# Opening the second feed-forward: seven-part chunks in place of two plain ones, and other places for the combinations of its input

## Chip, cores and metric

The kernel runs on one core of one Trainium2 chip. The metric is the device time of one execution in microseconds; the time before is the median of three runs.

## What is computed

A two-layer encoder over 768 tokens (two sequences, 512 and 256) with model width 1024, all in float32. Layer 0 mixes tokens by windowed attention, layer 1 by a gated width-3 convolution. Each layer then has the feed-forward that this change touches, and a gated input embedding:

```python
h = rms_norm(x, norm_mlp[i])
x = x + jnp.square(jax.nn.relu(h @ mlp_w_up[i])) @ mlp_w_down[i]
gate = jax.nn.sigmoid(rms_norm(x, norm_ple[i]) @ ple_w_gate[i])
x = x + (p[i] @ ple_w_proj[i]) * gate
```

Here i is the layer, mlp_w_up is 1024 x 4096 and mlp_w_down 4096 x 1024.

## The kernel before

**Precision.** Each float32 operand is split in two parts, a rounded high part (written by ScalarE, named ...hi) and the rest (written by VectorE as a subtraction, named ...lo). A product of two operands is three matmuls: high by high, high by low, low by high. So every tile of weights costs ScalarE a copy and VectorE a subtraction, and every input as well.

**Chunks and seven parts.** Tokens lie on the free axis in two halves of 384 (H). An up-projection chunk is a pair of weight tiles of 128 x 1024. Done plainly (plain_product), a chunk is 2 x 2 blocks of output by 8 blocks of depth by 3 matmuls, 96 matmuls of 128 x 384. Done in seven parts (seven_parts, a Winograd form of Strassen's scheme over 2 x 2 blocks), it is seven products of 12 matmuls, 84 in all. For that, sums of weights (Weights7: sums32, sums14) and of inputs are formed on VectorE. The inputs of the seven products are x11, x21 and x22 (blocks of the input) and t1 to t4 (their combinations). Plain chunks need x12 too, and no combinations. Norm7.block writes the x parts of one of the eight 128-row blocks m of the input, and Norm7.combine(m), m from 0 to 3, forms t1 to t4 of blocks m and m + 4: two copies q (ScalarE), four sums (t13, t42), two high parts t (ScalarE), two low parts t (VectorE).

**The norm.** h is x times a gain, times a reciprocal root per token (rstd). The gain is put in when the parts are made; rstd is applied after the matmuls. It needs acc, the sum of squares of all eight blocks: a split of acc (ah, al), four matmuls by ones (ss), logarithm, exponential, square and a Newton step. The logarithm needs another set of ScalarE's functions, so a table is loaded ahead of it (ACT_TABLE_LOAD, L647).

**Where the change lies.** In layer 1 the convolution ends with the output projection (project_add): eight products of 48 matmuls each, block order 0, 4, 1, 5, 2, 6, 3, 7. After each, VectorE adds it to x and Norm7.block runs for that block. first_chunk gives the function behind(i) that is called after each product: it fetches and splits the first weights of the feed-forward and runs combine for the first pairs of blocks. After the eighth product mlp takes the 16 up chunks u; two chunks make a group g, whose down products follow one chunk later. PLAIN = 2, 2 says that each layer's first two chunks are plain: they need no combinations, so the last two combine calls are run beside them (early = 2). Chunks 2 and later are in seven parts.

**Order.** The operations are recorded, and a planner with its own costs sets the order on each engine; each engine works through its list in that order. Tiles lie in numbered slots of the on-chip memory, which lists at the end of the program hand out (xs1, act1, spare, held1). Weights land in three shared tiles (wraw), the copies in two pairs (whi, wlo) and one more each (zhi/zlo, vhi/vlo). The names of products: in plain chunks p; in seven parts a, b, c and d, where c and d begin as ScalarE's copies of a. Each wlo, zlo and vlo is L874 on VectorE, each whi, zhi and vhi L863 on ScalarE.

Of the kernel before, what the change touches and what calls it, by code (L numbers as in the profile page):

```python
# [456 lines left out]
def trunk_kernel(ctx: ExitStack, tc: tile.TileContext, a: dict, out: bass.AP):  # L457
# [118 lines left out]
    def slot(i, name, dt=F32R, n=T):  # L576

        return home(slots if i < 32 else more, n, dt, f"S{i}", name)
# [20 lines left out]
    class Norm:  # L599
# [34 lines left out]
        aside = temp  # L634
# [80 lines left out]
    class Norm7(Norm):  # L715
# [2 lines left out]

        def __init__(self, i, name, places, aside, acc, rstd=None, apart=None):
            super().__init__(i, name, places, acc, rstd)  # L720
            self.free, self.x12 = list(places), list(aside)
            self.apart = self.free if apart is None else list(apart)
            self.xs = {k: {} for k in (*QS7.values(), "x12")}

# [3 lines left out]
        def block(self, m, xb):  # L728
            g = gain(self.i, m)
            if m < KB // 2:  # L730
                for j, t in enumerate((self.place(), slot(self.x12.pop(0), "x12"))):
                    src = xb[:, j * H : j * H + H]
                    hi, lo = t[:, :H], t[:, H:]
                    act.activation(hi, src, AF.Copy, scale=g)
                    dve.scalar_tensor_tensor(lo, src, g, hi.bitcast(F32), ALU.mult, ALU.subtract)
                    self.xs[("x11", "x12")[j]][m] = hi, lo
            else:
                hi, lo = self.place(), self.place()
                act.activation(hi[:], xb, AF.Copy, scale=g)
                dve.scalar_tensor_tensor(lo[:], xb, g, hi[:].bitcast(F32), ALU.mult, ALU.subtract)  # L740
                for j, k in enumerate(("x21", "x22")):
                    self.xs[k][m - KB // 2] = hi[:, j * H : j * H + H], lo[:, j * H : j * H + H]
            self.square(m, xb)
# [144 lines left out]
    def product7(ps, w, key, xs, start, step=P, col=0):  # L888

        hi, lo = w.w[key]  # L890
        rhs = xs[QS7[key]]
        ks = [(slice(step * i + col, step * i + col + P), rhs[i]) for i in range(512 // step)]
        terms = [(hi[:, c], p) for c, ps_ in ks for p in ps_] + [(lo[:, c], ps_[0]) for c, ps_ in ks]
        for i, (a, b) in enumerate(terms):
            pe.matmul(ps, lhsT=a, rhs=b, start=start and i == 0, stop=i == len(terms) - 1, skip_group_check=True)  # L895
# [242 lines left out]
    psum = ctx.enter_context(tc.tile_pool(name="ps", bufs=1, space=PSUM))  # L1138
# [724 lines left out]
    def up_chunk(l, u):  # L1863
        f = 4 * (u // 2) + u % 2
        return Weights7(a["up"][l, f], a["up"][l, f + 2], plain=u < PLAIN[l])


    PLAIN = 2, 2

    def run(steps, n=None):  # L1870

        for _ in range(len(steps) if n is None else n):
            steps.pop(0)()
# [31 lines left out]
        run(combined)  # L1905
        run(steps)

    def first_chunk(chunk, norm, early):


        w = []

        def behind(i):
            if i == 6:
                w.append(chunk(0))
                w[0].split("direct")
            if i == 7:
                w[0].split("second")
            if i % 2 and i // 2 < early:
                run(norm.combine(i // 2))  # L1920
            if i == 7:
                w.append(chunk(1))
                w[1].split("second")

        return w, behind

    ET = mybir.EngineType

# [65 lines left out]
        v.low("second")  # L1994
        return parts, v

    def seven_parts(w, xs, make, then, first, late, out, soon=False, apart=False):

        w.low("s32")
        w.split("s14")
        if not first:
            late()
        v = make()
        more7 = isinstance(v, Weights7)
        a = bank("A", "a")[:, :H]
        product7(a, w, "w11", xs, True)
        if not first:
            late()  # L2010
        c = bank("A" if first else "C", "c")[:, :H]
        act.activation(c, a, AF.Copy)
        if more7 and soon:
            v.sums32()
        late(3 if first else 1)
        w.split("w22")
        late()
        b = bank("A" if first else "B", "b")[:, :H]
        product7(b, w, "s3", xs, True)
        p = big("p")[:, :H]  # L2020
        act.activation(p, b, AF.Copy)
        if more7 and not soon:
            v.sums32()
        product7(a, w, "s2", xs, False)
        d = bank("B", "d")[:, :H]
        act.activation(d, a, AF.Copy)
        late(2)
        if more7:
            v.sums14(0 if apart else None)
            v.high("s32")  # L2030
        late()
        product7(c, w, "w12", xs, False)
        if more7:
            v.high("direct")
        product7(a, w, "s1", xs, False)
        out.y22(a, p)
        if more7 and apart:
            v.sums14(1)
# [33 lines left out]
    def mlp(l, norm, nxt, w, w1, places, early, spare, product=None, follow=None):  # L2072


        xs = norm.xs
        r = parts = None
# [55 lines left out]
        def late(n=1):  # L2132

            for _ in range(n):
                if pend:
                    pend.pop(0)()

        def up_plain(u, w, make, then):

            nonlocal r, parts  # L2140

            ps = [both(f"p{i + 1}", {0: "AA", 1: "BC"}.get(u, "AA")[i]) for i in range(2)]
            y1 = y2 = None
# [12 lines left out]
            for n, (i, ks, sides) in enumerate(plain_order(u or parts)):  # L2156
                plain_product(ps, w, xs, i, ks, sides)
                if n == 0:
                    if u:
                        v.split("direct")  # L2160
                        v.sums32()
                    elif product:
                        v.split("direct")
                        run(c[-1], 2)
                        norm.table()
                        ss = norm.sum_squares(psum, parts=parts, tag="C")
                    else:
                        parts = norm.acc_parts()
                        two(*c)
                        norm.table()  # L2170
                elif n == 1:
                    if u:
                        v.high("s32")
                        rects((0, 1), (0, 0))
                        v.low("s32")
                        v.sums14()
                        late(len(pend))
                    else:
                        if not product:
# [28 lines left out]
        def up(u, w, make, then):  # L2208

            out = Squares()  # L2210
            v = seven_parts(w, xs, make, then, u == PLAIN[l], late, out, u == PLAIN[l])
            pend.extend(acts_of(u, out.y1, out.y2, (out.y2, out.y1)))
            return v

# [727 lines left out]
    ls = [xs2[7]] + ys[:5] + [ys[7], ys[5]]  # L2942
    free = [i for i in xs2 if i not in hs + ls] + wide + [xs0[16], ys[6]]

    xs1 = free[:20] + hs
    act1 = ls[:7] + free[20:26] + ls[7:]

    n3 = Norm7(1, "mix1", xs2, x12, act0[9])
    w2, behind = first_chunk(conv_chunk, n3, 1)
    ple(n2, n3, act0[10:13], behind, w)  # L2950

    n4 = Norm7(3, "mlp1", xs1, act1[7:11], act1[11])
    w1, behind = first_chunk(lambda u: up_chunk(1, u), n4, 2)
    mixer_conv(n3, *w2, 1, n4, wide, xs0[16], ys, hs, ls, behind)
    spare = [xs1[i] for i in (17, 10, 11, 20, 0, 7, 14, 12, 13, 21, 22, 23, 24, 25)]
    held1 = [xs1[i] for i in (1, 2, 8, 9, 15, 16, 18, 19, 26, 27)] + act1[:2] + xs1[3:7] + act1[2:3]
    n5 = Norm(5, "ple1", held1[:16], held1[16])
    mlp(1, n4, n5, *w1, act1, 2, spare)
    free = act1[3:7] + act1[7:] + [spare[i] for i in (4, 11, 0, 1, 7, 8, 2, 3, 9, 10, 5, 6, 12, 13)]
    last_stage(  # L2960
        n5,
# [83 lines left out]
```

## Time and profile before

| | |
|---|---|
| median of 3 runs | 1625.18 us (1625.07 to 1625.44) |
| profiled execution, its own time | 1625.47 us |
| its span, first to last instruction | 1623.6 us |
| granted TensorE clock | 0.998 |
| busy share of the span: TensorE / VectorE / ScalarE / GpSimd | 99 / 84 / 58 / 6 % |

The profiled execution took 0.29 us more than the median, and 1.87 us of its time lie outside its span. In rows of the time line the columns are start, length, engine, line, operation, output and inputs, shapes, count, and in brackets the idle time before it and what ended it. PE is TensorE, PEld its loading of weights, DVE VectorE, ACT ScalarE, POOL GpSimd and SP the queue of transfers. Neighbouring instructions of one engine overlap a little, so two times matter: the length of a row, and its pace, which is the distance from its start to the start of the next row.

### The profile page before, as it was taken

The numbers are of one execution on the slowest core, as the hardware profiler recorded it, in microseconds if no ns is written. First come the engines' busy times: TensorE is split into PE (matmuls) and PEld (weight loads), VectorE is DVE, ScalarE is ACT, GpSimd is POOL, SyncE is SP. The second block draws the span as 40 slices with busy tenths as digits, with TensorE's granted clock in tenths as the row PEclk, the third lists the DMA queues.
The fourth block names the chain that finished last, engine by engine and source line by source line (L and its number), as shares of the span: only waits on it lengthen the run. The fifth ranks groups of instructions, "written<-read, shape, count | busy, mean of one in ns | idle before, by whom it ended". The sixth has DMA issues, their size and how long they took to land.

```text
span 1623.6 us, 24456 instructions
## 1 busy us (share of the span) xinstructions
PE 1613.7 (99%) x9325; PEld 1569.2 (97%) x9325; DVE 1368.3 (84%) x2225; ACT 946.6 (58%) x1497; POOL 99.5 (6%) x158
## 2 busy tenths in 40 slices
PE   9999999999999999999999999999999999999997
PEld 7988889999999999999999999999999999999987
DVE  7579988988888888998898777687888978889985
ACT  7478887655545555556663434565555545546655
POOL 0001000010110110100000000000110110010000
PEclk9999999999999999999999999999999999999999
DMA  8745312332443343323312211212343343342232
GB/s 305 204 131 152 98 37 88 114 91 82 114 108 95 97 103 94 103 70 103 104 62 78 70 69 70 78 66 67 100 106 93 103 106 86 94 117 78 84 121 88
DMA packets 61649, 163.71 MB, mean 101 GB/s; under 512 B 7611, under 2 KB 23355, under 8 KB 61532
## 3 DMA queue, kind: packets, MB, share of 16 engines
q1 hardware_dynamic: 47564, 143.14, 26.7%
q0 software_dynamic: 13824, 18.88, 7.1%
q8 instruction: 73, 1.20, 0.3%
q14 instruction: 44, 0.36, 0.1%
q10 hardware_dynamic: 144, 0.13, 0.0%
HBM read 123.85 MB, written 9.96 MB: 82 GB/s over the span
## 4 chain that ended last, share of the span: by engine, by line
PE 94%; DVE 3%; ACT 1%; issue 1%; DMA 0%; DVEq 0%; ACTq 0%
PE a L895 36%; PE b L895 9%; PE mm L435 9%; PE p L2064 6%; PE mm L557 6%; PE d L895 5%; PE c L895 5%; PE B L895 4%; PE C L895 4%; PE gate L2439 3%; PE O L435 2%; PE S L435 2%; PE gate L557 2%; PE pt L435 1%; PE vp L435 1%
## 5 line engine op out<-in xcount | busy, mean ns | idle before, releaser
L874 DVE TENSOR_TENSOR zlo<-sum,zhi 128x1024 fp32r<-128x1024 f32 x70 | 85.7, 1224 | 74.3 <-ACT zhi L863 74.1
L2271 POOL DMA_DIRECT2D x<-p x96 | 84.2, 878 | 976.5 <-DVE x L2232 779.7
L863 ACT ACTIVATE whi<-sum 128x1024 fp32r<-128x1024 f32 x70 | 74.4, 1063 | 103.8 <-PE a L895 92.6
L863 ACT ACTIVATE vhi<-wraw 128x512 fp32r<-128x512 f32 x70 | 44.3, 633 | 144.4 <-PE B L895 62.2
L895 PE MATMUL a<-xs,whi 128*128 128x384 f32 x608 | 117.6, 334 | 0.0
L895 PE MATMUL b<-t,zhi 128*128 128x384 f32 x560 | 113.6, 334 | 0.0
L895 PE MATMUL a<-t,zhi 128*128 128x384 f32 x560 | 113.5, 334 | 0.0
L895 PE MATMUL a<-t,whi 128*128 128x384 f32 x560 | 113.5, 334 | 0.0
L895 PE MATMUL a<-act,whi 128*128 128x384 f32 x512 | 109.3, 334 | 0.0
L895 PEld LDWEIGHTS a<-xs,whi 128*128 128x128 f32 x608 | 106.5, 188 | 0.0
L863 ACT ACTIVATE whi<-wraw 128x1024 fp32r<-128x1024 f32 x76 | 80.2, 1056 | 33.9 <-PE C L895 19.2
L895 PEld LDWEIGHTS b<-t,zhi 128*128 128x128 f32 x560 | 98.6, 188 | 0.0
L895 PEld LDWEIGHTS a<-t,zhi 128*128 128x128 f32 x560 | 98.5, 188 | 0.0
L895 PEld LDWEIGHTS a<-t,whi 128*128 128x128 f32 x560 | 98.5, 188 | 0.0
L863 ACT ACTIVATE zhi<-sum 128x1024 fp32r<-128x1024 f32 x70 | 74.3, 1062 | 39.6 <-PE a L895 37.0
L874 DVE TENSOR_TENSOR wlo<-wraw,whi 128x1024 fp32r<-128x1024 f32 x76 | 92.8, 1221 | 0.0
L895 PEld LDWEIGHTS a<-act,whi 128*128 128x128 f32 x512 | 90.6, 188 | 0.0
L874 DVE TENSOR_TENSOR wlo<-sum,whi 128x1024 fp32r<-128x1024 f32 x70 | 85.3, 1219 | 0.9 <-ACT whi L863 0.9
L435 PE MATMUL mm<-xs_mix,whi 128*128 128x512 f32 (+1 forms) x320 | 80.0, 339 | 0.0
L2232 DVE TENSOR_TENSOR x<-x,a 128x384 f32<-128x384 f32 x128 | 67.5, 549 | 12.0 <-PE a L895 12.0
L782 ACT ACTIVATE t<-y 128x768 fp32r<-128x768 f32 x64 | 53.6, 838 | 37.2 <-DVE y L778 22.2
L895 PE MATMUL a<-act,wlo 128*128 128x384 f32 x256 | 64.9, 334 | 0.0
(376 smaller groups left out, 4428.9 us busy)
## 6 DMA issues: line engine op xcount, KB each, us to landing
wraw<-in_up SPq DMA_DIRECT2D x64, 512.0 KB, 3.5
wraw<-in_down SPq DMA_DIRECT2D x64, 512.0 KB, 3.4
x<-p POOLq DMA_DIRECT2D x96, 192.0 KB, 3.0
wraw<-in_w_in SPq DMA_DIRECT2D x24, 512.0 KB, 3.4
wraw<-in_gate SPq DMA_DIRECT2D x16, 512.0 KB, 3.5
wraw<-in_w_q SPq DMA_DIRECT2D x8, 512.0 KB, 4.5
wraw<-in_w_out SPq DMA_DIRECT2D x8, 512.0 KB, 3.4
x_in<-in_x SPq DMA_DIRECT2D x8, 384.0 KB, 7.1
```

Of the source, the lines that this page charges most:

```text
L435: return f(*args, **kw)
L557: pe.matmul(t, lhsT=w, rhs=x[:, o:e], start=first and i == 0 and j == 0, stop=last and i == n - 1 and j == 2)
L782: act.activation(t[0][:], (self.q1, self.q2)[i][:], AF.Copy)
L863: act.activation(hi[:], src, AF.Copy)
L874: dve.tensor_tensor(lo[:], src, hi[:].bitcast(F32), ALU.subtract)
L895: pe.matmul(ps, lhsT=a, rhs=b, start=start and i == 0, stop=i == len(terms) - 1, skip_group_check=True)
L2064: pe.matmul(ps[i][o], lhsT=wt[:, c], rhs=xs[f"x{h + 1}{1 + o}"][m][part], start=k == 0 and j == 0, stop=k == KB - 1 and j == 2,)
L2232: dve.tensor_tensor(t[:, o : o + H], t[:, o : o + H], f, op)
L2271: pool.dma_start(low[i][:, o : o + H], p[:, i * H : i * H + H], accum_op=ALU.add)
L2439: pe.matmul(ps.t[:, o : o + n], lhsT=a_, rhs=b_, start=begin and i == 0 and j == 0, stop=end and i == len(terms) - 1 and j == 2,)
```

## The change

In the second layer the first two up chunks become seven-part chunks too (PLAIN = 2, 0). The combinations of block pairs 0, 1 and 2 are run during the output projection (early = 3), that of pair 3 after the first product of chunk 0 (the new function rooted, passed as opened), together with the norm's root. x12 is no longer made in this layer (aside = None), so four blocks have half as many parts to write. Only chunk 0's weights are prepared during the output projection, now with their sums; chunk 1 follows from inside chunk 0. The lists of slots are handed out anew.

```diff
         def __init__(self, i, name, places, aside, acc, rstd=None, apart=None):
             super().__init__(i, name, places, acc, rstd)
-            self.free, self.x12 = list(places), list(aside)
+            self.free, self.x12 = list(places), list(aside or ())
+            self.first = "x11", "x12"
+            if aside is None:
+                self.first = "x11",
...
-    PLAIN = 2, 2
+    PLAIN = 2, 0
...
-    def first_chunk(chunk, norm, early):
+    def first_chunk(chunk, norm, early, plain=True):
         w = []
+
+        def seven(i):
+            if i == 6:
+                w.append(chunk(0))
+            if i == 7:
+                w[0].sums32()
+                w[0].sums14()
+                w[0].high("s32")
+                w[0].split("direct")
+            if i % 2 and i // 2 < early:
+                run(norm.combine(i // 2))
...
-        return w, behind
+        return w, behind if plain else seven
...
         a = bank("A", "a")[:, :H]
         product7(a, w, "w11", xs, True)
+        if opened:
+            opened()
...
+        def rooted():
+
+            nonlocal r
+            for m in todo:
+                run(norm.combine(m))
+            sq = norm.acc_parts()
+            norm.table()
+            run(norm.rstd_steps(psum, norm.sum_squares(psum, parts=sq, tag="A")))
+            r = norm.r
...
-            v = seven_parts(w, xs, make, then, u == PLAIN[l], late, out, u == PLAIN[l])
+            first = u and u == PLAIN[l]
+            v = seven_parts(w, xs, make, then, first, late, out, first, opened=None if u else rooted)
...
-    xs1 = free[:20] + hs
-    act1 = ls[:7] + free[20:26] + ls[7:]
+    xs1 = free[:24] + hs[:4]
+    act1 = ls[:7] + hs[4:8] + free[24:26] + ls[7:]
...
-    n4 = Norm7(3, "mlp1", xs1, act1[7:11], act1[11])
-    w1, behind = first_chunk(lambda u: up_chunk(1, u), n4, 2)
+    n4 = Norm7(3, "mlp1", xs1, None, act1[11])
+    w1, behind = first_chunk(lambda u: up_chunk(1, u), n4, 3, False)
```

How the order moves is shown at three places. The numbers tell tiles of one name apart.

On TensorE, before, around the norm's sums in the first plain chunk: p_11087 and p_11090 are its two token halves, xs_11106 and xs_11116 the high and low part of the last input block, 7.

```order
L2064 MATMUL p_11087<-xs_11106,zhi 128x384
L2064 MATMUL p_11090<-xs_11106,zhi 128x384
L2064 MATMUL p_11087<-xs_11116,zhi 128x384
L2064 MATMUL p_11090<-xs_11116,zhi 128x384
L2064 MATMUL p_11087<-xs_11106,zlo 128x384
L2064 MATMUL p_11090<-xs_11106,zlo 128x384
L666 MATMUL ss<-ah,ones 128x384
L666 MATMUL ss<-al,ones 128x384
```

On TensorE now, at the same sums in chunk 0: t_11119 and t_11133 are the high and low part of pair 3's first combinations, t_11152 the high part of its second, xs_11126 and xs_11158 the parts of block 7.

```order
L899 MATMUL c<-xs_11126,whi 128x384
L666 MATMUL ss<-ah,ones 128x384 x2
L899 MATMUL b<-t_11133,zhi 128x384
L899 MATMUL b<-t_10672,zlo 128x384
L899 MATMUL b<-t_10817,zlo 128x384
L899 MATMUL b<-t_10974,zlo 128x384
L899 MATMUL b<-t_11119,zlo 128x384
L666 MATMUL ss<-al,ones 128x384 x2
L899 MATMUL a<-t_11152,zhi 128x384
L899 MATMUL c<-xs_11158,whi 128x384
```

The products b, a and c are no longer each in one piece: the matmuls that read pair 3 stand behind those that do not. 41 matmuls stand between the last one of the output projection and the one that reads t_11152.

On ScalarE, before, from the weights that wait for the last product of the output projection:

```order
L863 ACTIVATE whi<-wraw 128x1024
L626 ACTIVATE sq<-x 128x768
L739 ACTIVATE xs_11106<-x,vec 128x768
L498 ACTIVATE ah<-acc_mlp_10592 128x768
L647 ACT_TABLE_LOAD
L751 ACTIVATE q<-x,vec 128x768
L782 ACTIVATE t_11141<-q 128x768
L782 ACTIVATE t_11153<-q 128x768
```

And on ScalarE now, from the same place (whi of chunk 0's second sums) to the copy d:

```order
L867 ACTIVATE whi<-sum 128x1024
L755 ACTIVATE q<-x,vec 128x768
L626 ACTIVATE sq<-x 128x768
L2029 ACTIVATE c<-a 128x384
L786 ACTIVATE t_11119<-q 128x768
L743 ACTIVATE xs_11126<-x,vec 128x768
L498 ACTIVATE ah<-acc_mlp_10592 128x768
L647 ACT_TABLE_LOAD
L786 ACTIVATE t_11152<-q 128x768
L685 ACTIVATE ln<-ss,eps 128x384 x2
L867 ACTIVATE whi<-wraw 128x1024
L2038 ACTIVATE p<-b 128x384
```

The copies q and c and one part t now stand ahead of ah and of the table; the other part t stands right behind the table. After p come zhi<-sum and d<-a.

On VectorE, before, from the last addition to x:

```order
L1849 TENSOR_TENSOR x<-x,mm 128x384 x2
L874 TENSOR_TENSOR wlo<-wraw,whi 128x1024
L627 TENSOR_TENSOR acc_mlp_10592<-acc_mlp_10592,sq 128x768
L740 SCALAR_TENSOR_TENSOR xs_11116<-x,vec,xs_11106 128x768
L499 TENSOR_TENSOR al<-acc_mlp_10592,ah 128x768
L773 TENSOR_TENSOR q<-q 128x384
```

And on VectorE now, with one row ahead of that addition, a sum of chunk 1's weights:

```order
L840 TENSOR_TENSOR sum<-wraw 128x512
L1853 TENSOR_TENSOR x<-x,mm 128x384 x2
L878 TENSOR_TENSOR wlo<-sum,whi 128x1024
L777 TENSOR_TENSOR q<-q 128x384
L841 TENSOR_TENSOR sum<-sum,wraw 128x512
L627 TENSOR_TENSOR acc_mlp_10592<-acc_mlp_10592,sq 128x768
L781 SCALAR_TENSOR_TENSOR q<-q 128x384
L792 TENSOR_TENSOR t_11133<-q,t_11119 128x768
L782 SCALAR_TENSOR_TENSOR q<-q 128x384
L499 TENSOR_TENSOR al<-acc_mlp_10592,ah 128x768
L744 SCALAR_TENSOR_TENSOR xs_11158<-x,vec,xs_11126 128x768
L792 TENSOR_TENSOR t_11165<-q,t_11152 128x768
```

The combinations of pair 3 and a sum of weights now stand between the last addition and al. SP's list holds the same transfers in the same sequence. In the last stage of the program a few neighbouring instructions trade places (TensorE's transposes, and steps of the gates on VectorE and ScalarE).

More of the change, by code (lines that the diff above doesn't have):

```diff
@@ L730, in block @@
             if m < KB // 2:
-                for j, t in enumerate((self.place(), slot(self.x12.pop(0), "x12"))):
+                for j, k in enumerate(self.first):
+                    t = slot(self.x12.pop(0), k) if j else self.place()
                     src = xb[:, j * H : j * H + H]
@@ L735, in block @@
                     dve.scalar_tensor_tensor(lo, src, g, hi.bitcast(F32), ALU.mult, ALU.subtract)
-                    self.xs[("x11", "x12")[j]][m] = hi, lo
+                    self.xs[k][m] = hi, lo
             else:
@@ L1995, in ahead, with seven_parts @@
         return parts, v
-    def seven_parts(w, xs, make, then, first, late, out, soon=False, apart=False):
+    def seven_parts(w, xs, make, then, first, late, out, soon=False, apart=False, opened=None):
         w.low("s32")
@@ L2950, in trunk_kernel @@
     ple(n2, n3, act0[10:13], behind, w)
-    n4 = Norm7(3, "mlp1", xs1, act1[7:11], act1[11])
-    w1, behind = first_chunk(lambda u: up_chunk(1, u), n4, 2)
+    n4 = Norm7(3, "mlp1", xs1, None, act1[11])
+    w1, behind = first_chunk(lambda u: up_chunk(1, u), n4, 3, False)
     mixer_conv(n3, *w2, 1, n4, wide, xs0[16], ys, hs, ls, behind)
-    spare = [xs1[i] for i in (17, 10, 11, 20, 0, 7, 14, 12, 13, 21, 22, 23, 24, 25)]
-    held1 = [xs1[i] for i in (1, 2, 8, 9, 15, 16, 18, 19, 26, 27)] + act1[:2] + xs1[3:7] + act1[2:3]
+    spare = [xs1[i] for i in (21, 10, 11, 17, 0, 7, 14, 12, 13, 18, 19, 20, 24, 25)]
+    held1 = [xs1[i] for i in (1, 2, 8, 9, 15, 16, 22, 23, 26, 27)] + act1[:2] + xs1[3:7] + act1[2:3]
     n5 = Norm(5, "ple1", held1[:16], held1[16])
-    mlp(1, n4, n5, *w1, act1, 2, spare)
+    mlp(1, n4, n5, *w1, None, act1, 3, spare)
     free = act1[3:7] + act1[7:] + [spare[i] for i in (4, 11, 0, 1, 7, 8, 2, 3, 9, 10, 5, 6, 12, 13)]
```

## Prediction

> **What bounds the kernel now.** I read the page first: span, busy shares and the chain that ended last.
>
> ```profile
> span 1623.6 us, 24456 instructions
> PE 1613.7 (99%) x9325; PEld 1569.2 (97%) x9325; DVE 1368.3 (84%) x2225; ACT 946.6 (58%) x1497; POOL 99.5 (6%) x158
> PE 94%; DVE 3%; ACT 1%; issue 1%; DMA 0%; DVEq 0%; ACTq 0%
> ```
>
> The chain is TensorE for 94%. A busy TensorE need not be one at its pace, so I looked at the place itself: busy time by stretches, first the two plain chunks, then chunk 2, which is already in seven parts (columns: stretch, length, PE, PEld, DVE, ACT, POOL, clock, DMA share, GB/s).
>
> ```profile
> 1071.90:1105.90 34.00, 34.00 (x198) 34.00 (x197) 28.55 (x42) 19.38 (x25) 0.00 (x0) 1.00 0.19 62
> 1105.90:1120.40 14.50, 14.50 (x85) 14.50 (x84) 12.25 (x17) 8.53 (x12) 0.00 (x0) 1.00 0.12 37
> ```
>
> And TensorE's time line: the first matmul behind the output projection, and chunk 2's start.
>
> ```profile
> 1071.88 0.33 PE L2064 MATMUL p<-xs,zhi 128*128 128x384 f32 x1
> ...
> 1105.86 1.55 PE L895 MATMUL a<-xs,whi 128*128 128x384 f32 x8
> 1107.25 0.85 PE L895 MATMUL a<-xs,wlo 128*128 128x384 f32 x4
> 1107.94 1.37 PE L895 MATMUL b<-t,zhi 128*128 128x384 f32 x7
> ```
>
> Two plain chunks and the four matmuls ss, 196 matmuls, take 1105.86 - 1071.88 = 33.98 us, 0.1733 each; the twelve from 1105.86 to 1107.94 take 0.1733 each too. So TensorE does not wait here: what goes from its list is won, and what it comes to wait for is lost.
>
> **The change, part by part.** *TensorE.* Two chunks of 96 become two of 84: 24 matmuls less, 24 x 0.1733 = 4.16 us. That is the ceiling, since no wait of before is there to be removed. The Trainium skill's page "TensorE: Matmul & The Clock Gate" (Back-to-back issue gap) gives columns / 2.4 GHz + 2.5 ns, 162.5 ns at 384, by which the sum would be 3.9 us. The rows show 173.3 ns, and I take them.
>
> *VectorE and ScalarE, totals.* A chunk's weights cost VectorE two subtractions of 1024 before; now four sums of 512 and subtractions of 3584 columns. Its eviction was four of 384; now four of 384 and one of 768. Four x12 parts of 384 go. The paces, from starts in the ScalarE and VectorE time lines (the chain behind the last addition, then single rows):
>
> ```profile
> 1071.73 1.06 ACT L863 ACTIVATE whi<-wraw 128x1024 fp32r<-128x1024 f32 x1 [3.12 <-PE mm L557]
> 1072.95 0.85 ACT L626 ACTIVATE sq<-x 128x768 f32<-128x768 f32 x1 [0.16 <-DVE x L1849]
> 1073.70 0.92 ACT L739 ACTIVATE xs<-x,vec 128x768 fp32r<-128x768 f32 x1
> 1074.95 0.85 ACT L498 ACTIVATE ah<-acc_mlp 128x768 fp32r<-128x768 f32 x1 [0.33 <-DVE acc_mlp L627]
> 1075.82 1.28 ACT L647 ACT_TABLE_LOAD   x1
> 1077.12 0.94 ACT L751 ACTIVATE q<-x,vec 128x768 f32<-128x768 f32 x1
> ...
> 1082.33 1.05 ACT L685 ACTIVATE ln<-ss,eps 128x384 f32<-128x384 f32 x2 [0.60 <-DVE v L683]
> ```
>
> ```profile
> 1040.42 0.92 ACT L751 ACTIVATE q<-x,vec 128x768 f32<-128x768 f32 x1
> 1041.25 0.93 ACT L739 ACTIVATE xs<-x,vec 128x768 fp32r<-128x768 f32 x1
> ...
> 1108.47 0.47 ACT L2012 ACTIVATE c<-a 128x384 f32<-128x384 f32 x1
> 1108.88 0.83 ACT L782 ACTIVATE t<-y 128x768 fp32r<-128x768 f32 x1
> ...
> 1111.61 1.06 ACT L863 ACTIVATE zhi<-sum 128x1024 fp32r<-128x1024 f32 x1 [0.89 <-PE a L895]
> 1112.58 0.47 ACT L2026 ACTIVATE d<-a 128x384 f32<-128x384 f32 x1
> ```
>
> ```profile
> 1071.90 1.02 DVE L1849 TENSOR_TENSOR x<-x,mm 128x384 f32<-128x384 f32 x2 [2.03 <-PE mm L557]
> 1072.83 1.22 DVE L874 TENSOR_TENSOR wlo<-wraw,whi 128x1024 fp32r<-128x1024 f32 x1
> 1073.97 0.95 DVE L627 TENSOR_TENSOR acc_mlp<-acc_mlp,sq 128x768 f32<-128x768 f32 x1
> 1074.84 1.01 DVE L740 SCALAR_TENSOR_TENSOR xs<-x,vec,xs 128x768 fp32r<-128x768 f32 x1
> ...
> 1088.09 0.68 DVE L836 TENSOR_TENSOR sum<-wraw 128x512 f32<-128x512 f32 x1
> 1088.69 0.69 DVE L842 TENSOR_TENSOR sum<-wraw 128x512 f32<-128x512 f32 x1
> ```
>
> VectorE's pace is 1.14 for 1024 columns (1072.83 to 1073.97), 0.87 for 768, 0.60 for 512 and 0.47 for 384. So a chunk adds 4 x 0.60 + 3 x 1.14 + 0.60 + 0.87 - 2 x 1.14 = 5.0 us, two add 10.0, less 4 x 0.47 for x12: some 8 us more. While TensorE is not kept waiting this costs nothing; the rows above leave VectorE 5.4 us idle beside the plain chunks, and its idle time in the output projection takes chunk 0's sums and pair 2's combination. ScalarE is busy 19.38 of 34.00 and has room. GpSimd shows nothing there.
>
> *The opening, where TensorE now waits.* Before, plain products covered the last block's parts, the last two combinations and the norm. Now 41 matmuls stand ahead of the one that reads t_11152: it is due at 1071.88 + 41 x 0.1733 = 1078.99. ScalarE's list up to it, by paces: whi 1071.73; q of block 7 must follow the addition to x and starts 1072.95, where sq did; sq 1073.78 (q's pace, 0.83); c 1074.53 (0.75); t_11119 1074.94 (0.41); xs 1075.69; ah 1076.52; table 1077.39 (0.87); t_11152 1078.69 (1.30), ready at 1079.54. VectorE keeps up with it: wlo to 1073.97, then q 1073.97, sum 1074.44, acc 1075.04 to 1075.99, q 1075.91, t 1076.38, q 1077.30 to 1077.85, all before their readers. How a hand-over to TensorE and a wait are paid shows a wait of before, in an earlier stage:
>
> ```profile
> 832.15 1.02 DVE L740 SCALAR_TENSOR_TENSOR xs<-x,vec,xs 128x768 fp32r<-128x768 f32 x1
> ...
> 832.39 0.51 PE L2064 MATMUL p<-xs,zhi 128*128 128x384 f32 x2
> 833.22 0.62 PE L2064 MATMUL p<-xs,zhi 128*128 128x384 f32 x2 [0.32 <-DVE xs L740]
> 833.68 0.51 PE L2064 MATMUL p<-xs,zlo 128*128 128x384 f32 x2
> ```
>
> 0.05 us from xs (ready 833.17) to the matmul, and two matmuls then take 0.46 instead of 0.35, so 0.11 more. Hence TensorE goes on at 1079.59: 0.60 + 0.11 lost. Queued behind the waiting matmul are the rest of a, c and then chunk 1's first product, which all wait with it.
>
> *The second wait.* From 1079.70, 11 matmuls end chunk 0's a and c (1081.61), and nine of chunk 1's first product follow (1083.17); its whi is ready at 1081.52. The next needs d, the copy of a: ScalarE does ln from 1079.44 (1.02), whi 1080.46 (0.97), p 1081.43 (0.41), zhi 1081.84 (0.97), d 1082.81, ready 1083.28, for TensorE 1083.33. That is 0.16 + 0.11 lost. Together 0.98 us. As bounds I take 0 (the planner's order covers all) and 0.98 + 1.28 (a further table's length on the chain).
>
> The Trainium skill's page "ScalarE: Activation LUTs" (What ACT_TABLE_LOAD costs) adds about 1380 ns of drain to each load's 1283 ns. The rows show the load's 1.28 us and the next copy 1.30 us after its start, so no drain. By the page the opening would lose 1.38 us more and the sum would be 1.8 us.
>
> *Later.* Only evictions ask for the root, and the banks that they free are next written two chunks on, in a seven-part chunk as before. The tightest place is chunk 2's last product, which must not overwrite a before VectorE's row y<-a,p has read it. From the last addition to that row VectorE has 61 instructions (9 of 1024, 14 of 768, 13 of 512, 25 of 384): 10.26 + 12.18 + 7.80 + 11.75 = 41.99 us, from 1071.90 to 1113.89. TensorE comes there after 244 matmuls at 1071.88 + 42.29 + 0.98 = 1115.15. 1.26 us are left for VectorE's own waits; priced at nothing.
>
> *Transfers and the last stage.* SP's list is unchanged. One VectorE sum of chunk 1's weights stands ahead of the last addition to x, and everything above waits behind it. Its later tile is freed by chunk 0's wlo, which stands behind the seventh product as the first row here did.
>
> ```profile
> 1064.52 1.22 DVE L874 TENSOR_TENSOR wlo<-wraw,whi 128x1024 fp32r<-128x1024 f32 x1
> ...
> wraw<-in_up SPq DMA_DIRECT2D x64, 512.0 KB, 3.5
> 1542.80:1595.00 52.20, 52.20 (x239) 42.81 (x238) 41.00 (x60) 27.02 (x43) 0.00 (x0) 1.00 0.30 97
> ```
>
> The tile is free at 1065.74, its transfer lands 3.5 us later, 1069.2, while the sum is due by 1071.2: 2.0 us of cover; what is later than that is lost in full. In the last stage (third row) neighbours trade places beside a full TensorE: nothing; if that cover were gone, one piece of VectorE, under 1 us.
>
> *Sum.* 4.16 - 0.98 = 3.18 us. The profiled execution, 1625.47, would take 1622.3; the median, 0.29 lower, 1622.0.
>
> **Rivals.** *A, nothing waits.* The planner moved matmuls that need pair 3 to the back, and the walk's waits are small. For it: no lost time in any row of this stage. Against: the chain of ScalarE is 0.60 us too long by its own rows. 1625.18 - 4.16 = 1621.0.
>
> *B, a longer chain to t_11152.* Eight ScalarE steps in a row, each handed over by another engine; one more wait of a table's length, 1.28 us, or weights that land late, goes straight to TensorE: 1622.0 + 1.3 = 1623.3. Against: the chain of before shows hand-overs of 0.03 us (addition to sq). The drain in the Trainium skill's page named above would be such a wait, and the row of the load speaks against it.
>
> *C, VectorE becomes the bound (slower).* The place is y<-a,p of chunk 2. 41.99 us hold only if instructions overlap as above; a row is 0.08 to 0.09 longer than its pace (1.22 against 1.14). If none overlaps, since each waits for ScalarE or TensorE, 61 x 0.09 = 5.5 us come on top, 1.26 are covered, 4.2 pass to TensorE: 1622.0 + 4.2 = 1626.2. It decides from (1.26 + 3.18) / 61 = 0.07 us on each instruction. Against: VectorE's rows here overlap in whole runs.
>
> *D, the change does not do it*: the saving is eaten by moved instructions elsewhere. The order shows 24 matmuls less and the rest of TensorE's list the same, so hardly.
>
> **How the numbers follow.** Forecast (waits of 0.5 to 1.5 us) 0.55, A 0.15, B 0.22, C 0.06, D 0.02. About 0.2%, 3.25 us, is what a measurement of this kernel can tell from no change; the forecast, 3.18 us or 0.196%, lies at that line. Faster by more: A and half of the forecast, 0.42. Within: the other half, B, D and a little of C, 0.52. Slower by more: 0.06. The range goes from A's 1621.0, with 0.1 for the spread of the runs, to past B, 1624.2.
>
> **What would show it.** In the changed profile: 84 matmuls for each of the two chunks; TensorE idle once ahead of a<-t behind the table, some 0.6 us, and once ahead of the product that needs d, some 0.2; no idle time from chunk 1's second product on. If the idle time stands at y<-a,p or at a weight's lo part, C is right; if ahead of the sums of weights, the transfers; if there is none, A. A sum of idle times over 2.3 us would prove the walk wrong.

## The result

| | before | changed |
|---|---|---|
| median | 1625.65 us (17 runs, 1624.89 to 1627.56) | 1622.09 us (17 runs, 1621.74 to 1623.04) |
| profiled execution, its own time | 1625.47 us | 1621.74 us |
| its span | 1623.6 us | 1619.9 us |

The ratio of the changed kernel to the one before is 0.9978, 95% interval 0.9971 to 0.9986: 3.56 us or 0.22% less, predicted 3.18 us (1622.0) and a range of 1620.9 to 1624.2. The middle lies just past the line of 0.2% at which the forecast lay, the interval on both sides of it. The page of the changed kernel opens with

```profile
span 1619.9 us, 24420 instructions
PE 1609.5 (99%) x9301; PEld 1564.1 (97%) x9301; DVE 1373.6 (85%) x2235; ACT 948.5 (59%) x1503; POOL 99.8 (6%) x158
```

24 matmuls less than the 9325 of before, 10 VectorE and 6 ScalarE instructions more. The two chunks by stretches, from the first matmul behind the output projection to chunk 2, and chunk 2 itself (columns as in the prediction):

```profile
1071.48:1102.15 30.67, 30.47 (x173) 29.70 (x173) 30.55 (x44) 22.41 (x32) 0.00 (x0) 1.00 0.15 52
1102.15:1116.71 14.56, 14.56 (x85) 14.56 (x85) 14.37 (x23) 9.59 (x15) 0.00 (x0) 1.00 0.21 73
```

The stretch took 33.98 us before and takes 30.67 now: 3.31 us won. 172 matmuls at 0.1733 us make 29.81, so 0.86 us are lost to waits, where the prediction had 0.98. The rest of the 3.73 us between the two profiled executions is that TensorE reaches the stretch at 1071.48 instead of 1071.88, behind instructions that the change doesn't touch; that 0.40 us is not explained by the change. 0.28 us of it arise at 833 us, at the wait for xs that the prediction shows (0.59 us lost there before, 0.32 now), and in the traces of the other kernels with the same first layer TensorE enters the stretch anywhere between 1071.62 and 1072.78 us. From chunk 2 on the distance between the two executions stays the same, so nothing is given back later. VectorE is now busy 30.55 of 30.67 us.

Where the 0.86 us go is seen in TensorE's time line. A lost time is the distance between the starts of two rows, less 0.1733 for each matmul of the first:

```profile
1071.48 1.55 PE L899 MATMUL a<-xs,whi 128*128 128x384 f32 x8
...
1073.56 1.21 PE L899 MATMUL b<-t,zhi 128*128 128x384 f32 x6
1074.72 1.14 PE L899 MATMUL a<-t,zhi 128*128 128x384 f32 x5
1075.70 0.33 PE L899 MATMUL b<-t,zhi 128*128 128x384 f32 x1
...
1078.49 0.52 PE L666 MATMUL ss<-al,ones 128*128 128x384 f32 x2
1079.21 0.44 PE L899 MATMUL a<-t,zhi 128*128 128x384 f32 x1 [0.20 <-ACT t L786]
1079.49 0.34 PE L899 MATMUL c<-xs,whi 128*128 128x384 f32 x1
...
1082.82 1.65 PE L899 MATMUL a<-t,whi 128*128 128x384 f32 x8
1084.30 0.85 PE L899 MATMUL a<-t,wlo 128*128 128x384 f32 x4
```

0.12 us ahead of the first a<-t,zhi and 0.11 within its five; 0.37 ahead of the one that needs t_11152 (the profile's idle time shows only 0.20 of it) and 0.11 at the matmul behind it; 0.09 within the eight of chunk 1's first rows a<-t,whi, where the copy d lands; 0.81 in all; the other 0.05 are distances too small to place. ScalarE's list up to these places:

```profile
1072.62 0.94 ACT L755 ACTIVATE q<-x,vec 128x768 f32<-128x768 f32 x1 [0.23 <-DVE x L1853]
1073.46 0.83 ACT L626 ACTIVATE sq<-x 128x768 f32<-128x768 f32 x1
1074.20 0.47 ACT L2029 ACTIVATE c<-a 128x384 f32<-128x384 f32 x1
1074.61 0.82 ACT L786 ACTIVATE t<-q 128x768 fp32r<-128x768 f32 x1
1075.34 0.93 ACT L743 ACTIVATE xs<-x,vec 128x768 fp32r<-128x768 f32 x1
1076.17 0.83 ACT L498 ACTIVATE ah<-acc_mlp 128x768 fp32r<-128x768 f32 x1
1077.02 1.28 ACT L647 ACT_TABLE_LOAD   x1
1078.31 0.85 ACT L786 ACTIVATE t<-q 128x768 fp32r<-128x768 f32 x1
1079.06 1.03 ACT L685 ACTIVATE ln<-ss,eps 128x384 f32<-128x384 f32 x2
```

ScalarE works without a gap from the last addition to x on. Shifted by the 0.40 us, each row stands within 0.1 us of the prediction's walk: t_11152 forecast at 1078.69, found at 1078.31. And VectorE's list beside it:

```profile
1071.51 1.02 DVE L1853 TENSOR_TENSOR x<-x,mm 128x384 f32<-128x384 f32 x2 [3.70 <-PE mm L557]
...
1074.07 0.68 DVE L841 TENSOR_TENSOR sum<-sum,wraw 128x512 f32<-128x512 f32 x1
1074.67 0.95 DVE L627 TENSOR_TENSOR acc_mlp<-acc_mlp,sq 128x768 f32<-128x768 f32 x1
...
1078.21 1.01 DVE L744 SCALAR_TENSOR_TENSOR xs<-x,vec,xs 128x768 fp32r<-128x768 f32 x1
1079.19 0.96 DVE L792 TENSOR_TENSOR t<-q,t 128x768 fp32r<-128x768 f32 x1
...
1113.72 0.55 DVE L2223 TENSOR_TENSOR y<-a,p 128x384 f32<-128x384 f32 x1
```

Two things to keep for the experiments: a sum of chunk 1's weights (L841) stands in the midst of the last pair's work, and the row y<-a,p of chunk 2 ends at 1114.27, 0.36 us before TensorE comes there (1102.15 + 72 x 0.1733 = 1114.63).

### The profile page after: what moved, and what is told of

It is laid out like the page before. It is cut to its first block, busy times and chain, and to the rows that moved or that the text cites. A ratio compares the mean times of both kernels' runs of the same rounds, so it can differ in the third digit from the quotient of the medians.

```text
span 1619.9 us, 24420 instructions
## 1 busy us (share of the span) xinstructions
PE 1609.5 (99%) x9301; PEld 1564.1 (97%) x9301; DVE 1373.6 (85%) x2235; ACT 948.5 (59%) x1503; POOL 99.8 (6%) x158
## 4 chain that ended last, share of the span: by engine, by line
PE 97%; DVE 2%; ACT 1%; issue 0%; DMA 0%; SPq 0%; DVEq 0%; ACTq 0%
PE a L899 37%; PE b L899 9%; PE mm L435 8%; PE mm L557 6%; PE d L899 5%; PE c L899 5%; PE p L2081 4%; PE gate L557 4%; PE B L899 4%; PE C L899 4%; PE gate L2467 3%; PE O L435 2%; PE S L435 2%; PE pt L435 1%; PE vp L435 1%; PE pj L1977 1%
## 5 line engine op out<-in xcount | busy, mean ns | idle before, releaser
L899 PE MATMUL a<-xs,whi 128*128 128x384 f32 x640 | 123.8, 334 | 0.0
L899 PE MATMUL a<-t,zhi 128*128 128x384 f32 x576 | 117.3, 334 | 0.2 <-ACT t L786 0.2
L899 PE MATMUL b<-t,zhi 128*128 128x384 f32 x576 | 117.0, 334 | 0.0
L899 PEld LDWEIGHTS a<-xs,whi 128*128 128x128 f32 x640 | 112.1, 188 | 0.0
L899 PE MATMUL a<-xs,wlo 128*128 128x384 f32 x320 | 68.3, 334 | 0.0
```

## The experiments

Each kernel is given against the runs of the kernel before in its own set (medians 1625.79, 1626.03 and 1625.93 us); the changed kernel stands at -3.56 us. "Lost" is what TensorE's time line shows between 1070 and 1130 us by the sum above, from distances of 0.04 us on; the changed kernel has 0.81 there.

| kernel | median, us | against before | ratio, 95% interval | lost, us |
|---|---|---|---|---|
| no_table | 1622.17 | -3.62 | 0.9970 to 0.9988 | 0.73 |
| longer_t | 1623.17 | -2.62 | 0.9975 to 0.9993 | 1.48 |
| x12_kept | 1622.55 | -3.24 | 0.9972 to 0.9989 | 0.92 |
| no_table_sums | 1621.70 | -4.33 | 0.9963 to 0.9984 | 0.24 |
| sums_behind | 1621.92 | -4.11 | 0.9963 to 0.9984 | 0.24 |
| seven_both | 1624.52 | -1.27 | 0.9985 to 1.0002 | 0.69, and 6.4 in layer 0 |
| layer0_one | 1621.05 | -4.98 | 0.9956 to 0.9981 | 0.82, and 1.0 in layer 0 |
| one_plain | 1623.99 | -1.94 | 0.9979 to 0.9997 | 0.25 |
| vector_work | 1622.51 | -3.52 | 0.9969 to 0.9987 | 0.78 |
| vector_work6 | 1623.44 | -2.49 | 0.9975 to 0.9993 | 1.62 |
| both | 1620.11 | -5.82 | 0.9952 to 0.9977 | 0.25, and 1.0 in layer 0 |

The intervals are 2.8 to 4.1 us wide, so smaller differences between two kernels are read from the lost times, and the medians only say whether they agree. Each of these kernels was ordered anew by the planner, so an edit can also move instructions that it does not name; where that matters it is said.

**longer_t: is ScalarE's chain what TensorE waits for?**

(The condition is written out in words.)

```diff
-            act.activation(t[0][:], (self.q1, self.q2)[i][:], AF.Copy)
+            for _ in range(2 if last_pair_of_mlp1 else 1):
+                act.activation(t[0][:], (self.q1, self.q2)[i][:], AF.Copy)
```

> The changed kernel with one more ScalarE instruction: the high part t_11152 of the last pair is written twice with the same values (pace of that row 0.75 us). Theory: ScalarE's chain is what TensorE waits for, so the 0.75 us pass to the time in full: the wait ahead of a<-t_11152 grows from 0.37 to about 1.1 us, and the time to 1622.8 to 1622.9. Rival 1 (the planner's order of TensorE leaves other matmuls that could run there, or the wait belongs to another engine): 0 to 0.3 us more. Rival 2 (VectorE, 0.36 us from holding TensorE up in chunk 2, also waits for t and falls behind): up to 0.75 us passes there as well only if TensorE had not been late by as much already, so again no more than 0.75.

TensorE's row at that place:

```profile
1079.71 0.51 PE L666 MATMUL ss<-al,ones 128*128 128x384 f32 x2
1081.16 0.45 PE L900 MATMUL a<-t,zhi 128*128 128x384 f32 x1 [0.94 <-ACT t L787]
```

The wait is 1.10 us (1081.16 - 1079.71 - 0.35) where it was 0.37: of the 0.75 us added, 0.73 pass on. ScalarE's list there:

```profile
1078.12 0.83 ACT L787 ACTIVATE t<-q 128x768 fp32r<-128x768 f32 x1
1078.97 1.28 ACT L647 ACT_TABLE_LOAD   x1
1080.26 0.84 ACT L787 ACTIVATE t<-q 128x768 fp32r<-128x768 f32 x1
```

ScalarE works without a gap here too, and TensorE goes on 0.06 us after the second t ends (1081.10), so the chain's end decides, as expected, and there was no slack in it. The two copies of t stand on both sides of the table: the planner had VectorE do q earlier, ahead of a low part of t, so that the first copy could come ahead of the table. The median went up by 0.94 us, of which the lost time explains 0.67.

**no_table: taking the largest step out of that chain.**

```diff
     n4 = Norm7(3, "mlp1", xs1, None, act1[11])
+    n4.ready = True
```

> The changed kernel without the table load of this norm (the set that the previous norm loaded is still the one in use, so the result is the same). Theory: TensorE's longest wait in the opening, 0.37 + 0.11 us ahead of a<-t_11152, ends when ScalarE's chain whi, q, sq, c, t, xs, ah, table, t ends. Without the table's 1.28 us t is ready 1.28 us earlier, before TensorE asks for it, and the copy d comes earlier by as much, so that its 0.09 us goes too. The 0.12 + 0.11 us at the copy c and the next product stay. So 0.4 to 0.6 us less than the changed kernel: 1621.5 to 1621.7 us against 1622.1, and no ACT_TABLE_LOAD in that stage. Rival (t only comes last by chance, VectorE's low parts and sums of the same pair end almost as late): the wait stays for another releaser, 0 to 0.2 us less.

```profile
1077.84 0.85 ACT L786 ACTIVATE t<-q 128x768 fp32r<-128x768 f32 x1 [0.53 <-DVE q L782]
1079.24 1.06 ACT L685 ACTIVATE ln<-ss,eps 128x384 f32<-128x384 f32 x2 [0.56 <-PE ss L666]
```

```profile
1078.53 1.01 DVE L744 SCALAR_TENSOR_TENSOR xs<-x,vec,xs 128x768 fp32r<-128x768 f32 x1
...
1079.15 0.34 PE L899 MATMUL a<-t,zhi 128*128 128x384 f32 x1
1079.60 0.45 PE L899 MATMUL c<-xs,whi 128*128 128x384 f32 x1
```

The rival was right. The wait ahead of a<-t is gone, and at the very next matmul, which reads VectorE's xs (ready at 1079.54), stands one of 0.28 + 0.11 us. ScalarE now waits 0.53 us for VectorE's q. The lost time at the copy d, which was expected to go, stays at 0.11 us: ScalarE's ln waits 0.56 us for ss, so that d comes only 0.13 us earlier after TensorE's entry, and TensorE as much. 0.06 us won by the medians, 0.08 by the rows, out of 1.28 us taken away: two chains ended almost together, and only one was shortened. The run also corrects what was said of the norm at the start: this logarithm needs no other set of functions, since the previous norm's load, at 835.75 us in the changed kernel, had brought the same one (both loads are L647) and no load stands between the two.

**no_table_sums and sums_behind: the other chain.** The four sums of chunk 1's weights are issued behind the last low part of pair 3.

```diff
-        if more7 and not soon:
-            v.sums32()
+        if opened:
+            with record.issue_after(last_low_of_pair_3):
+                v.sums32()
```

(sums14 alike; the name of the instruction waited for is written out in words.) no_table_sums has the edit of no_table as well.

> The kernel without the table load, and in addition the four sums of chunk 1's weights are held back on VectorE until the last low part of pair 3 is written (one of them stood among that pair's work). Theory (two chains end almost together: without the table, ScalarE's t comes 0.8 us earlier, but VectorE's xs and t low parts, with a sum of 0.60 us ahead of them, then hold TensorE for 0.28 + 0.11 us, nearly what the table had cost): with the sum out of the way too the wait goes, 0.4 us less than without the table alone: about 1621.7 us, and no idle time of over 0.15 us in the opening. Rival (the sums are due in chunk 1, and held back they are late for zhi): the 0.4 us come back, or more, as a wait ahead of the products with zhi in chunk 1: 1622.1 to 1623.

> The changed kernel with its table load, and the four sums of chunk 1's weights held back as in no_table_sums. Theory (ScalarE's chain ends last, VectorE's by less than 0.1 us earlier): the wait of 0.37 + 0.11 us ahead of a<-t_11152 stays as it is, the time is that of the changed kernel, 1622.1 within 0.2. Rival (VectorE was the one that held TensorE up): 0.4 us less, 1621.7.

no_table_sums came out at 1621.70 us as expected: only the 0.24 us at c and behind it are left. In sums_behind my theory fell: the wait ahead of a<-t was expected to stay and went altogether, again with 0.24 us left at c. ScalarE's list there shows why.

```profile
1077.26 0.83 ACT L498 ACTIVATE ah<-acc_mlp 128x768 fp32r<-128x768 f32 x1
1078.00 0.83 ACT L788 ACTIVATE t<-q 128x768 fp32r<-128x768 f32 x1
1078.85 1.28 ACT L647 ACT_TABLE_LOAD   x1
1080.14 1.06 ACT L869 ACTIVATE whi<-wraw 128x1024 fp32r<-128x1024 f32 x1
```

(TensorE enters this execution's opening at 1072.58, 1.10 us later than in the changed kernel, so that t at 1078.00 answers to 1076.90 there.) VectorE's row of q, which t copies, in the changed kernel:

```profile
1076.87 0.55 DVE L782 SCALAR_TENSOR_TENSOR q<-q 128x384 f32<-128x384 f32 x1
```

and in sums_behind:

```profile
1076.63 0.55 DVE L784 SCALAR_TENSOR_TENSOR q<-q 128x384 f32<-128x384 f32 x1
```

From TensorE's entry to the start of q it is 5.39 us there and 4.05 here. Without the sum, and with a low part of t behind q instead of ahead of it, q is ready 1.3 us earlier, and the planner puts t ahead of the table load instead of behind it. So one VectorE sum of 0.60 us had stood in two ways: ahead of VectorE's own low parts, and, in the order that the planner chose with it, with t behind 1.28 us of table. Neither the table nor the sum alone is "the" cause of the 0.37 us; moving the sum removes it, with or without the table. Nor does the sum force t behind the table: in longer_t it keeps its place, and q starts 4.51 us after TensorE's entry, since there the low part of t follows q. What decides is when VectorE has q ready. The sums were not missed in chunk 1: no wait showed there.

**x12_kept: is leaving out x12 worth anything?**

```diff
-    n4 = Norm7(3, "mlp1", xs1, None, act1[11])
+    n4 = Norm7(3, "mlp1", xs1, act1[7:11], act1[11])
```

> The changed kernel, in which the four x12 parts are written as before, though nothing reads them: four ScalarE copies (0.5 us pace) and four VectorE subtractions (0.47 us) more, all during the output projection. Theory: both engines wait for TensorE there after every product (2 to 5 us at a time in the time line), so the parts cost nothing: 1622.1 within 0.2 us, and the edit that drops them is worth nothing. Rival: the last block's x12 stands ahead of the opening's chain and delays t_11152: 0.4 to 0.5 us more, in the wait ahead of a<-t_11152.

Little or nothing: the lost time is 0.92 instead of 0.81, since one of the four copies falls between whi and q and moves the copy c, and with it the first wait from 0.12 to 0.29 us (some of it comes back at d). The wait ahead of a<-t_11152, which the rival named, is 0.35 + 0.12 us, as without the copies. The median is 0.32 us higher, above the 0.2 that was expected, but less than these runs can tell.

**one_plain: half the change.** Only the second chunk in seven parts.

```diff
-    PLAIN = 2, 2
+    PLAIN = 2, 1
```

(with chunk 1's sums behind the first one's norm.)

> The kernel before, in which only the second chunk of the second layer becomes a seven-part chunk (the first stays plain, x12 and the order of the pairs stay). Theory (a plain chunk in front covers the last two pairs, the norm and the root, so half the matmuls are won without the opening's waits): 12 x 0.1733 = 2.08 us less than before, with no idle time of TensorE over 0.15 us, about 1.5 us behind the changed kernel's 3.56. Rival (as in the first layer with one plain chunk, whose opening lost 1.0 of 2.08 us: the pairs and chunk 1's four sums together are too much beside one plain chunk): 1.0 to 1.4 us less than before.

1.94 us less than before, 0.25 us lost, at chunk 1's first product b alone: 2.08 - 0.25 = 1.83. What holds b up there was not looked into. A plain chunk in front does hide the last two pairs, the norm and the root. Dropping the second plain chunk costs 0.25 of its 2.08 us; the 0.81 us of the changed kernel come with dropping the first as well.

**seven_both and layer0_one: the same in the first layer.** seven_both has the edit of no_table and PLAIN = 0, 0; layer0_one is the changed kernel with PLAIN = 1, 0.

> The kernel without that table load, and in the first layer too both plain chunks become seven-part chunks (pair 3 and the root behind the first product, chunk 0's sums of weights ahead of it; x12 there is still written). Theory (what decides is the work between the last norm input and the first matmul that needs the last pair): in the first layer the products of the embedding stand between the norm and chunk 0, so the pairs are ready earlier and 24 x 0.1733 = 4.16 us are won nearly whole: about 1617.5 us, 4.0 us below the kernel without the table. Rival 1 (each opening loses 0.5 to 1 us whatever stands ahead): 3.2 to 3.7 us below it, 1618.1. Rival 2 (the sums of weights and the copies of the embedding's products collide on VectorE and ScalarE): under 2 us below it, over 1619.5.

> The changed kernel, in which the first layer opens with one plain chunk in place of two (its second chunk in seven parts). Theory (the first plain chunk gives the cover for the pairs' combinations and the root; the second gives none, so it is 12 matmuls for nothing): 12 x 0.1733 = 2.08 us less than the changed kernel, 1620.0 us, with no idle time of TensorE in the first layer's opening. Rival (the first layer is short of VectorE there, as its opening without any plain chunk, which lost 6.1 us, showed): the sums for chunk 1, 2.4 us, and the combinations take the plain chunk's cover, and 0.5 to 2 us are lost: 1620.5 to 1622.

In the first layer the theory failed. seven_both is 2.35 us above no_table where 4.0 below was expected. TensorE's rows in that opening:

```profile
290.08 1.11 PE L899 MATMUL b<-t,zhi 128*128 128x384 f32 x4
291.90 0.44 PE L899 MATMUL b<-t,zhi 128*128 128x384 f32 x1 [0.71 <-DVE t L792]
292.30 0.79 PE L899 MATMUL a<-t,zhi 128*128 128x384 f32 x3
292.93 0.34 PE L899 MATMUL c<-xs,whi 128*128 128x384 f32 x1
294.45 0.45 PE L899 MATMUL b<-t,zhi 128*128 128x384 f32 x1 [1.19 <-ACT t L786]
294.85 0.62 PE L899 MATMUL a<-t,zhi 128*128 128x384 f32 x2
296.19 0.58 PE L899 MATMUL b<-t,zhi 128*128 128x384 f32 x1 [0.72 <-DVE t L792]
```

When chunk 0 starts there (286.95 us), VectorE still has all the low parts of t of three pairs to write, not of one, and ScalarE carries out the copies of the embedding's products (pjs) as well. TensorE waits for one pair after another, 6.4 us in all by the starts of its rows, against 4.16 saved: here a pair that was not combined ahead of the chunk was paid for in the open. With one plain chunk the loss is 1.0 of 2.08 us, the rival's answer, and the median is 1.42 us below the changed kernel's.

**vector_work and vector_work6: is VectorE the bound?** Sums that are due in chunk 2 are written three times (four instructions, 2.4 us more) and six times (6.0 us).

```diff
-            v.sums14(0 if apart else None)
+            for _ in range(1 + again):
+                v.sums14(0 if apart else None)
```

> The changed kernel with 2.4 us more work for VectorE in chunk 1: two of the sums of weights (512 columns, pace 0.60 us) are written three times with the same values. By the trace of the changed kernel VectorE works 29.61 of 29.70 us beside the two chunks, and its row y<-a,p of chunk 2 ends 0.36 us ahead of TensorE: 2.4 - 0.36 = 2.0 us pass to TensorE, as idle time in chunk 1 or 2: 1624.1 us. By the margin that the prediction worked out, 1.26 us, 1.1 us would pass: 1623.2. Rival (VectorE runs ahead of its readers by far, its full share is work that isn't due): no change, 1622.1.

> The changed kernel with 6.0 us more work for VectorE in chunk 1 (the two sums of weights written six times with the same values). 2.4 us passed without a trace: the planner put the repeats among work that is due later, and VectorE gave the time back by 1145 us. Theory: VectorE has 11.41 of 14.00 and 13.14 of 15.00 us busy in the two stretches behind chunk 2, so some 4.4 us can be put off until there and 1 to 2 us pass to TensorE: 1623 to 1624 us. By the point that the prediction gave for VectorE as the bound (slower than before from 1.26 + 3.18 = 4.4 us), 6.0 - 1.26 = 4.7 us would pass: 1626.8. Rival (work can be put off for longer still): no change, 1622.1 to 1622.5.

2.4 us left no trace in TensorE's list, which has the waits of the changed kernel and no other: the rival's answer. With 6.0 us the time fell into the range that was expected, but not by the mechanism: the loss of 1.62 us stands in the opening, ahead of chunk 1, where the planner now has ScalarE do xs ahead of t and the copy c, and TensorE waits for these two (t is ready at 1076.00 and the matmul that reads it starts at 1076.05); none of it is a wait for VectorE. Busy time by stretches, of the changed kernel and then of vector_work6:

```profile
1086.00:1101.50 15.50, 15.50 (x92) 15.50 (x91) 15.47 (x25) 9.13 (x14) 0.00 (x0) 1.00 0.27 98
1101.50:1116.00 14.50, 14.50 (x85) 14.50 (x84) 14.31 (x22) 9.75 (x14) 0.00 (x0) 1.00 0.19 67
1116.00:1130.00 14.00, 14.00 (x83) 14.00 (x82) 11.41 (x18) 8.00 (x12) 0.87 (x1) 1.00 0.24 84
1130.00:1145.00 15.00, 15.00 (x89) 15.00 (x88) 13.14 (x21) 7.89 (x12) 3.50 (x4) 1.00 0.55 128
```

```profile
1086.00:1101.50 15.50, 15.50 (x91) 15.50 (x90) 15.47 (x26) 8.65 (x13) 0.00 (x0) 1.00 0.18 65
1101.50:1116.00 14.50, 14.50 (x86) 14.50 (x85) 14.37 (x23) 9.62 (x14) 0.00 (x0) 1.00 0.22 74
1116.00:1130.00 14.00, 14.00 (x83) 14.00 (x82) 13.79 (x22) 7.18 (x12) 0.87 (x1) 1.00 0.23 77
1130.00:1145.00 15.00, 15.00 (x88) 15.00 (x87) 14.78 (x24) 8.97 (x14) 3.24 (x4) 1.00 0.52 122
```

In the first two stretches VectorE was full already and stays so; the added work appears in the third and fourth, where it fills VectorE's idle time (4.0 of the 6.0 us in these two). So the full share beside chunks 1 and 2 was work taken early, and it can be put off. These kernels were ordered anew with the added work in them; what the fixed order of the changed kernel would bear was not tried.

**both: the edits that paid, together.**

> The changed kernel with three edits together: no table load in the second layer's norm, chunk 1's sums of weights held back there, and one plain chunk instead of two in the first layer. Theory (the openings lie 780 us apart and don't touch each other): the gains add up. Against the kernel before 4.33 us by the second layer's two edits and 1.0 to 1.4 us by the first layer: 5.3 to 5.7 us less, 1620.3 to 1620.7 by a before of 1626.0. Rival (slots and transfers are shared, and the planner places both anew): under 5.0 us.

1620.11 us, 5.82 us below before, ratio 0.9964 (0.9952 to 0.9977), a little more than the sum expected, by less than the interval's width. It is the fastest kernel of this study, 2.26 us further below before than the changed one.

## Why the prediction was right

*TensorE, 4.16 us.* Right: 24 matmuls less, and the pace unchanged at 0.1733 us. The Trainium skill's page "TensorE: Matmul & The Clock Gate" (Back-to-back issue gap) gives the formula that the prediction took from it for an isolated matmul, and says itself that a stream of weight loads and matmuls, which this is, goes at another pace; the 3.9 us by it are an estimate. The rows of both kernels show 173.3 ns at 384 columns.

*The opening wait, 0.60 + 0.11.* The mechanism was right and longer_t shows it: ScalarE's chain up to t_11152 ends last and passes on whatever is added. The size was right as a sum only. The rows have 0.37 + 0.11 there, and 0.12 + 0.11 earlier, at the copy c, which the prediction had in its list of ScalarE (1074.53) without asking who waits for it: TensorE, whose next product a needs the copy done. TensorE came to t_11152 0.23 us later for that, so the wait there is shorter by as much: 0.71 in all, as forecast. That is not luck: the end of ScalarE's chain sets when TensorE goes on, whatever it waited for before. What the prediction did not see is why t stood behind the table: the sum of weights in VectorE's list, which its walk has at 1074.44 among what is done "all before their readers". With ScalarE's order given that was so; sums_behind and longer_t show that the order hangs on when VectorE has q. And it treated the chain as one; no_table shows a second, VectorE's, less than 0.1 us behind (in the changed kernel t is ready at 1079.16 and xs at 1079.22).

*The second wait, 0.16 + 0.11.* Too large: 0.09 was found, and no wait ahead of the row. d was ready at 1082.76 by its row (1082.26 + 0.50), forecast 1083.28 - 0.40 = 1082.88, and TensorE came to it at 1082.82. This term, 0.27 us in the sum, is what sets the 0.98 us forecast apart from the 0.81 found.

*Later, priced at nothing.* Right in the price: no wait behind chunk 1's first product. The margin at y<-a,p was 0.36 us, not 1.26: VectorE's list up to the end of that row's pace took 42.68 us (1071.51 to 1114.19) where the walk had 41.99. Rival C's condition, that VectorE is the bound from 0.07 us per instruction on, 4.4 us in all, did not bear out as it was put: 6.0 us more work made no wait for VectorE, in a list that was ordered anew with it. The walk took the order of VectorE's list as fixed and a small margin at one row as the engine's slack; what stood ahead of that row was partly work for later.

*Transfers.* Right in the price, by a wrong walk: the sum of chunk 1's weights ran at 1067.12, before the last addition, and VectorE then waited 3.70 us for TensorE, for no transfer. That is 2.1 us ahead of the landing at 1069.2 that the walk had for the sum's later tile. The transfer into the tile that chunk 0's wlo frees was issued at 1065.37 and cannot have been the one, as landings take 3.3 to 3.5 us here; the two before it were issued at 1053.57 and 1057.05, so the cover was larger than the 2.0 us reckoned.

*Rivals.* A (nothing waits) is ruled out by the rows, 0.81 us lost. B (1.28 us more on the chain) did not happen; the load and its neighbour take 1078.31 - 1077.02 = 1.29 us. The Trainium skill's page "ScalarE: Activation LUTs" (What ACT_TABLE_LOAD costs) adds a drain of about 1380 ns for every switch to a different set. This load is no such switch, so it alone can't tell; but the load at 835.75 us in the changed kernel is one, behind the sigmoids of the gate (L2388, with their own load at 778.43), and there too the next row, the logarithm, starts at 837.04, 1.29 us later, without a drain. D is ruled out by 3.31 us in that very stretch.

*The line at 0.2%.* The forecast of 3.18 us lay 0.07 us short of it, the median 0.31 past it. With 0.12 us of the difference from the waits, the rest lies within the spread of the runs: the 0.40 us of the profiled execution ahead of the stretch are of that kind.

## What to carry to other kernels

Ahead of a change that takes cover away, walk each engine's list from the last input to the first reader, and ask of every instruction in it whether it belongs there: here holding back the next chunk's sums, of which one of 0.60 us stood in the way, won 0.57 us of lost time, and leaving out a 1.28 us table load alone won 0.08, because the other engine's chain ended less than 0.1 us behind. The same change won 3.3 us with one pair of inputs left to combine and lost 2.3 us with three, so count what is left behind the last input before copying it to the next layer. A share of 99% on a second engine is no bound while part of it is work taken early: 6.0 us more of it, in a list ordered anew, made TensorE wait for VectorE nowhere.

## What the runs showed of the hardware

A table load for a set that is already in place takes its full 1.28 us on ScalarE (row at 1077.02, the same length as the load at 835.75 that does change the set); in no_table, without it, the logarithm's row takes 1.06 us as against 1.03 with it. In the second layer's opening of the changed kernel, longer_t, no_table, x12_kept and sums_behind, each wait of TensorE is followed by 0.11 to 0.12 us more within the next few matmuls, also where the wait itself is only 0.07 or 0.12 us; why, no run shows. The profile's bracket does not show that part, nor all of the wait (0.20 for 0.37), so that lost time is better read from the starts.
